# Splitting the activations of a second feed-forward product where they are made, in a hybrid decoder layer on one core

## The chip, the core and the metric

The kernel runs on one core of a Trainium2 chip. The metric is the device time of one execution in microseconds (us). Before the change it is 1844.94 us, the median of three runs (1843.99 to 1846.52).

The engines that matter here are TensorE (PE in the profile, with its weight loads PEld), VectorE (DVE), ScalarE (ACT), GpSimd (POOL) and SyncE (SP), which here issues nearly all transfers, in the order of its instructions.

## The reference, cut to what matters

One decoder layer on 1024 tokens of width 1024: two mixers, a merge, and a SwiGLU feed-forward block with 2816 hidden units, in float32. The change touches only the end of the layer:

```python
x = x + SwiGLU(rms_norm(x))      # (silu(h @ w_gate) * (h @ w_up)) @ w_down
return rms_norm(x)
```

Products are computed to nearly float32 accuracy: each float32 operand is split into two parts of 12 bits, `src = hi + lo`, and TensorE computes hi·hi + hi·lo + lo·hi.

## The kernel before, in words

The order of TensorE's instructions is the order of the code. The order on VectorE, ScalarE, GpSimd and SyncE is laid out by a scheduler when the program is built (but for a stretch ahead of the feed-forward block that is written out by hand), from its own estimates of durations; on the chip each engine goes through its list strictly in order, each instruction waiting for its semaphores.

*Splitting.* `split(hi, lo, src)` (L79) is two instructions: ScalarE writes `hi` (L81), then VectorE subtracts, `lo = src - hi` (L82).

*Gate and up.* The loop `for f in range(NF_)` (L1529) makes 22 tiles of 128 hidden units. Each takes seven products of quarters (Strassen and Winograd), in the order 1, 6, 2, 7, 4, 5, 3. A product is 12 matmuls: four pieces, and for each of them three matmuls (L143 to L145), of which the third takes `alo`, the rest of the split operand. `prepare` splits the operand of a product two products ahead; `ahi` and `alo` have three buffers each. VectorE sums the results; the activations of a tile are `act[0]` (L1547) and `act[1]` (L1559), halves of the tokens. Two tiles make a pair. At the end of the even tile GpSimd computes S3 = A11 - A21 (L1567), at the end of the odd one S1, S2 and S4 (L1571 to L1573; S2 reads S3). Then SyncE stores the seven operands of the second product, 1: A11, 2: A12, 3: S4, 4: A22, 5: S1, 6: S2, 7: S3, as float32 to `act_d` in DRAM (L1575).

*The second product.* `down(p)` (L1610) is called for p = 1, 2, 3, 6, 5, 7, and a last part does p = 4; each has 11 pieces `k` of 12 matmuls. For a piece, `a_load` (L1457) brings the activations back (a transfer of 512 KB holds two pieces, three buffers `raw`), and two splits follow: of the activations (`ahi`, `alo`) and of w_down's quarter (`act` buffers). The loads of w_down (`w_load`, L1451) stand in the same queue. The quarters of w_down are also combined: VectorE forms B12 - B11 in place (L1590), GpSimd the other sums (`psub`, L87, and L1595). The results are added to the rows of x by VectorE and GpSimd between the pieces.

Of the kernel before, what the change touches and what calls it, by code (L numbers as in the profile page):

```python
# [11 lines left out]
F32 = mybir.dt.float32  # L12
# [8 lines left out]
P = 128  # L21
S = 1024
D = 1024
NT = S // P            # token tiles
KD = D // P            # contraction tiles of the model width
H = 4                  # delta-net heads
# [3 lines left out]
SEG0 = 2056            # first column of the sparse-attention part of w_in  # L30
# [3 lines left out]
def tile_hybrid(ctx: ExitStack, tc: tile.TileContext, a: dict, out: bass.AP, dbg=None):  # L34
# [13 lines left out]
    # ------------------------------------------------------------ constants and pools of the whole kernel  # L48
# [18 lines left out]
    # per head a square of 128 x 128, at a pitch by which its blocks of 16 x 16 on the diagonal are evenly spaced  # L67
# [10 lines left out]
    # ------------------------------------------------------------ helpers  # L78
    def split(hi, lo, src):  # L79
        """src = hi + lo, each of 12 bits"""  # L80
        nc.scalar.activation(hi, src, AF.Copy)  # L81
        nc.vector.tensor_tensor(lo, src, hi.bitcast(F32), op=ALU.subtract)  # L82
# [19 lines left out]
    def load_w(parts, cols, spare=False):  # L102
        """parts: (k0, k1, c0, c1, DRAM AP [p1 - p0, k, c], p0, p1) of a piece [128, 8, cols]; its (hi, lo)"""
# [18 lines left out]
    # pieces of weights in the order of their use, each loaded while the one before it is in use  # L122
# [17 lines left out]
    def mmk(ps, a_, b_, first, last):  # L140
        """ps += a^T b of split operands (hi, lo)"""
        (ah, al), (bh, bl) = a_, b_
        nc.tensor.matmul(ps, ah, bh, start=first, stop=False)  # L143
        nc.tensor.matmul(ps, ah, bl, start=False, stop=False)  # L144
        nc.tensor.matmul(ps, al, bh, start=False, stop=last)  # L145
# [10 lines left out]
    def rms_scale(p, src, nfeat, junk):  # L156
        """(mean square + eps)^-0.5 of each row of src [128, n]"""
# [7 lines left out]
    def to_feature_major(ptile, src, dst):  # L165
        """rows of a token tile [128, 1024] into columns; dst(kk) gives (hi, lo) of four feature tiles"""
# [9 lines left out]
    class Model:  # L176
        """rough times of the engines, for the order of TensorE's work"""
# [5 lines left out]
        def run(self, eng, ready, dur):  # L183
            """the end of dur ns of work that can begin at ready; TensorE goes in order, the others where they have time"""
# [16 lines left out]
    def weave(m, streams, filler=None, oldest=False):  # L201
        """emit the streams' steps, of those that can begin first (the one that waits longest, where oldest);
        a stream asks with the time its step is ready"""
# [26 lines left out]
    def steps(m, gen):  # L230
        """a stream of steps that give their (time, time until the next is ready); None: not yet"""
# [12 lines left out]
    # ------------------------------------------------------------ the order of the weights  # L244
# [19 lines left out]
    # ============================================================ phase 1: projections and the delta net  # L264
# [36 lines left out]
    # ---------------- the normed input, and z, beta, alpha: token major  # L301
    with ExitStack() as px:
# [16 lines left out]
        def zproj(s, i, wh, wl):  # L319
# [11 lines left out]
            # twice the silu; the half of it comes with the norm  # L331
# [42 lines left out]
    # ---------------- constants of the delta net  # L374
    upper = gt("upper", [P, P])                       # upper[t, i] = 1 where t <= i
# [7 lines left out]
    # blocks of 16 rows are inverted one by one, then level l joins blocks of b = 2^l rows:  # L383
    # LM[i, l - 4, c] = 1 where i is in an odd block, c in the even one before
    LM = gt("LM", [P, 3, P])
    for l in range(4, 7):
# [4 lines left out]
        # p >= 2 b m + b  # L391
        nc.gpsimd.affine_select(out=v, in_=src, pattern=[[-2 * b, nb], [0, 2 * b]], compare_op=ALU.is_ge,
                                fill=0.0, base=-b, channel_multiplier=1)
        # p < 2 b m + 2 b
        nc.gpsimd.affine_select(out=v, in_=v, pattern=[[2 * b, nb], [0, 2 * b]], compare_op=ALU.is_gt,
                                fill=0.0, base=2 * b, channel_multiplier=-1)
        # c in the even block
# [8 lines left out]
    # ---------------- beta, log decay and its running sum, all tokens at once  # L406
# [13 lines left out]
    # softplus(x) = max(x, 0) + log1p(e), e = exp(-|x|); log1p(e) = 2 artanh(e / (2 + e))  # L420
# [21 lines left out]
    # ---------------- q, k, v of the delta net: feature major, convolution and SiLU (twice its value)  # L442
# [31 lines left out]
    # its columns as rows, to be spread over all partitions  # L474
# [8 lines left out]
    # ---------------- delta net, a chunk of 128 tokens at a time  # L483
# [11 lines left out]
    EV = 1750                        # ns from a step's products to the next step of its chain  # L495

    def prepare_chunks():
        for c in range(NT):
# [4 lines left out]
            # decay: gb[., h, i] = gc_i on every partition  # L503
# [42 lines left out]
            # back to feature major  # L546
# [24 lines left out]
            # A[j, i] = L[i, j] and (q k^T)^T, both with the decay  # L571
# [12 lines left out]
            # the blocks on the diagonal: rows of Y = (I + U)^-1 from the last, U[a, b] the block of A  # L584
# [43 lines left out]
    def scan_chunks():  # L628
        Sst = None
        for c in range(NT):  # L630
# [36 lines left out]
            # gated norm of the heads, transposed  # L667
# [30 lines left out]
    # ---------------- the other projections: sparse attention's token major, merge gates feature major  # L698
# [28 lines left out]
    # ============================================================ phase 2: sparse attention  # L727
    # with the gates and the delta net's branch set in where TensorE would wait
# [6 lines left out]
    KT = [kvt(f"KT{g}", [P, 2, S], F32R) for g in range(2)]      # rows (hi | lo) of the two branches  # L735
    VS = [kvt(f"VS{i}", [P, 2, 2, P], F32R) for i in range(NT)]  # [token, branch, g, halves]
    KCS = kvt("KCS", [P, 2, 64], F32R)                           # rows (hi | lo); [g, block]
# [985 lines left out]
```

## Time and profile before

| | |
|---|---|
| time, median of three runs | 1844.94 us (1843.99 to 1846.52) |
| span of the profiled execution | 1843.4 us |
| TensorE busy | 1731.2 us, 94% |
| VectorE busy | 1201.9 us, 65% |
| ScalarE busy | 786.5 us, 43% |
| GpSimd busy | 794.5 us, 43% |
| mean granted TensorE clock | 0.982 |

The time of the profiled execution is its span, from the first instruction to the last, and a little around it; the timed runs lie 0.6 to 3.1 us above the span. The profile's TensorE line in 40 slices is 9 or more nearly everywhere, so the few slices that are not are where time can be won, and any new wait of TensorE in a slice at 9 is lost time. The second product runs from 1604.41 to 1836.15 us in the trace; what follows are the last sums, the last norm and the stores.

### The profile page before, as it was taken

Reading aid. Unit: us, or ns where it says so; the run is one execution under the profiler, and the core shown is the slowest. Engines: PE = TensorE matmul, PEld = TensorE weight load, DVE = VectorE, ACT = ScalarE, POOL = GpSimd, SP = SyncE. Lnnn points to the kernel's source line nnn. Section 1 sums busy time; section 2 is a strip of 40 time slices with the busy share of each in tenths; the row PEclk is TensorE's granted clock in tenths of the full one; section 3 lists DMA queues with packets and bytes.
Section 4 is the critical chain, followed back from the end, with each engine's and each line's share of the span. In section 5 each row is a group of like instructions: output and inputs, shape, how many; then the busy total and the mean of one; then the engine's idle time right before and its main releaser. Section 6 shows DMA issues by size and latency. Waiting matters only on the chain.

```text
span 1843.4 us, 26137 instructions
## 1 busy us (share of the span) xinstructions
PE 1731.2 (94%) x9252; PEld 1449.0 (79%) x9252; DVE 1201.9 (65%) x2084; ACT 786.5 (43%) x1852; POOL 794.5 (43%) x1118
## 2 busy tenths in 40 slices
PE   7999989999999999999999977799999999989998
PEld 7888888988877777877778756578888888877776
DVE  6566466665443687776734598975555555678985
ACT  5244333433221897877721124433333333334452
POOL 3410243443132875765510564644444343354720
PEclk9999999999999999999999999899999999999999
DMA  6323434443463211011085520033333332662232
GB/s 203 98 92 98 137 115 110 113 124 83 115 189 97 80 47 49 20 44 38 16 262 140 201 84 1 12 115 111 95 103 114 96 111 91 211 240 87 86 136 99
DMA packets 182947, 196.41 MB, mean 107 GB/s; under 512 B 23344, under 2 KB 139296, under 8 KB 182816
## 3 DMA queue, kind: packets, MB, share of 16 engines
q1 hardware_dynamic: 164048, 162.03, 28.7%
q0 software_dynamic: 18560, 32.62, 5.9%
q8 instruction: 73, 1.20, 0.3%
q14 instruction: 58, 0.48, 0.1%
q10 hardware_dynamic: 208, 0.09, 0.0%
HBM read 139.01 MB, written 55.69 MB: 106 GB/s over the span
## 4 chain that ended last, share of the span: by engine, by line
PE 62%; DVE 13%; issue 12%; POOL 6%; ACT 3%; DMA 3%; SPq 0%; POOLq 0%; DVEq 0%; ACTq 0%
PE M L144 13%; PE M L145 12%; PE M L143 12%; PE s L1068 3%; PE ppt L1126 3%; DVE alo L82 2%; PE po L1153 2%; PE po L1154 2%; DVE Ut L592 1%; PE pm L143 1%; PE pm L144 1%; PE pm L145 1%; POOL Ps L1103 1%; PE py L623 1%; DMA E<-gc_d 1%
## 5 line engine op out<-in xcount | busy, mean ns | idle before, releaser
L1073 ACT ACTIVATE Ps<-s,mx 128x384 f32<-128x384 f32 (+3 forms) x192 | 106.1, 561 | 23.5 <-DVE mx L1072 22.4
L81 ACT ACTIVATE ahi<-fraw 128x512 fp32r<-128x512 f32 x88 | 55.7, 633 | 140.5 <-PE M L144 140.5
L82 DVE TENSOR_TENSOR ptl<-ppt,pth 128x512 fp32r<-128x512 f32 (+1 forms) x148 | 99.0, 683 | 25.5 <-ACT pth L81 25.1
L1103 POOL TENSOR_SCALAR Ps<-Ps,cs 128x384 f32<-128x384 f32 (+3 forms) x192 | 108.3, 582 | 13.2 <-ACT pth L81 5.5
L1072 DVE TENSOR_REDUCE mx<-s 128x1 f32<-128x384 f32 (+3 forms) x192 | 95.0, 514 | 19.1 <-PE s L1071 13.5
L1068 PE MATMUL s<-KT,qt 128*128 128x384 f32 (+3 forms) x384 | 99.3, 359 | 3.0 <-DVE ptl L82 1.8
L143 PE MATMUL pn<-whi,h 128*128 128x264 f32 (+1 forms) x320 | 100.4, 314 | 1.1 <-ACT nst L706 1.1
L143 PE MATMUL pm<-h,whi 128*128 128x512 f32 x224 | 97.2, 434 | 0.2 <-ACT thm L719 0.2
L81 ACT ACTIVATE pth<-ppt 128x512 fp32r<-128x512 f32 (+1 forms) x148 | 87.1, 604 | 23.8 <-PE ppt L1126 21.6
L144 PE MATMUL pn<-wlo,h 128*128 128x264 f32 (+1 forms) x320 | 90.9, 284 | 0.0
L145 PE MATMUL pn<-whi,h 128*128 128x264 f32 (+1 forms) x320 | 90.9, 284 | 0.0
L144 PE MATMUL M<-act,ahi 128*128 128x512 f32 x194 | 78.7, 406 | 12.8 <-DVE act L82 12.8
L145 PE MATMUL pm<-h,wlo 128*128 128x512 f32 x224 | 89.7, 400 | 0.0
L144 PE MATMUL pm<-h,whi 128*128 128x512 f32 x224 | 89.2, 398 | 0.0
L82 DVE TENSOR_TENSOR alo<-fraw,ahi 128x512 fp32r<-128x512 f32 x88 | 73.6, 836 | 22.9 <-ACT ahi L81 22.9
L82 DVE TENSOR_TENSOR wlo<-wraw,whi 128x1024 fp32r<-128x1024 f32 (+1 forms) x50 | 61.1, 1232 | 41.9 <-ACT whi L81 40.2
L81 ACT ACTIVATE ahi<-fsum 128x512 fp32r<-128x512 f32 x66 | 41.8, 633 | 105.7 <-PE M L144 105.7
L82 DVE TENSOR_TENSOR alo<-ar,ahi 128x512 fp32r<-128x512 f32 x66 | 68.2, 1033 | 26.6 <-ACT ahi L81 26.6
L81 ACT ACTIVATE ahi<-ar 128x512 fp32r<-128x512 f32 x66 | 41.7, 631 | 100.1 <-PE dn L144 50.7
L81 ACT ACTIVATE whi<-wraw 128x1024 fp32r<-128x1024 f32 (+1 forms) x50 | 52.2, 1060 | 70.7 <-PE pm L144 31.1
L1126 PE MATMUL ppt<-ident,Ps 128*128 128x128 f32 x528 | 77.7, 273 | 1.4 <-POOL Ps L1103 1.1
L145 PE MATMUL M<-act,alo 128*128 128x512 f32 x194 | 76.6, 395 | 0.0
(518 smaller groups left out, 5741.2 us busy)
## 6 DMA issues: line engine op xcount, KB each, us to landing
wraw<-in_w_in_dram SPq DMA_DIRECT2D x50, 512.0 KB, 4.2
fraw<-in_w_gate_up_dram SPq DMA_DIRECT2D x44, 512.0 KB, 4.2
ar<-act_d SPq DMA_DIRECT2D x35, 512.0 KB, 3.5
act_d<-asum SPq DMA_DIRECT2D x44, 256.0 KB, 2.4
act_d<-act SPq DMA_DIRECT2D x33, 256.0 KB, 2.0
gt_d<-thm POOLq DMA_DIRECT2D x32, 256.0 KB, 3.0
gg<-gt_d SPq DMA_DIRECT2D x32, 256.0 KB, 2.7
qkv_d<-ac POOLq DMA_DIRECT2D x24, 256.0 KB, 2.3
```

Source lines behind the costliest of these rows:

```text
L81: nc.scalar.activation(hi, src, AF.Copy)
L82: nc.vector.tensor_tensor(lo, src, hi.bitcast(F32), op=ALU.subtract)
L143: nc.tensor.matmul(ps, ah, bh, start=first, stop=False)
L144: nc.tensor.matmul(ps, ah, bl, start=False, stop=False)
L145: nc.tensor.matmul(ps, al, bh, start=False, stop=last)
L1068: nc.tensor.matmul(s, qt[:, h, l, :], KT[g][:, b, j0 * P + c0:j0 * P + c1], start=l == 0, stop=l == 1 and not ext)
L1072: nc.vector.tensor_reduce(mx[:, h, n:n + 1], s, axis=AX.X, op=ALU.max, negate=True)
L1073: nc.scalar.activation(pr, s, AF.Exp, bias=mx[:, h, n:n + 1], accum_out=sums[:, h, n:n + 1])
L1103: nc.gpsimd.tensor_scalar(v, v, cs[:, h, n:n + 1], 1.0, op0=ALU.mult, op1=ALU.mult)
L1126: nc.tensor.transpose(pt[:k, h, :], prs[h][:, jj * P:jj * P + k], ident)
L1153: nc.tensor.matmul(po, v, th_, start=first, stop=False)
L1154: nc.tensor.matmul(po, v, tl_, start=False, stop=fin is not None)
```

## The change

The seven operands are split when they are made. `a_store(p, t)` writes `hi` to a new tile `ahs` (two buffers), `lo` in the place of the float32 operand, and stores both: two transfers of 256 KB for each operand instead of one. Operand 1 is split and stored at the end of the even tile, the other six at the end of the odd tile, in the order 7, 5, 6, 4, 3, 2. In the second product `a_load` brings both halves of one piece in one transfer of 512 KB, and the split of the activations is gone; w_down's halves now use the buffers `ahi` and `alo`. For the last product the halves are loaded straight into the big tiles. `act` has four buffers instead of six. The comments of the file were taken out as well.

```diff
-    act_d = {p: [dtile(f"act_d{p}_{k}", [P, 2, 512]) for k in range(0, NK, 2)] for p in range(1, 8)}
+    act_d = {p: [dtile(f"act_d{p}_{k}", [P, 2, 512]) for k in range(NK)] for p in range(1, 8)}
...
     def a_load(p, k):
-        if (p, k // 2) not in ars:
-            m = min(2, NK - k)
-            t = fw.tile([P, KD, P], F32, tag="raw", name="ar", bufs=3).rearrange("p (m k) t -> p m (k t)", m=2)
-            nc.sync.dma_start(t[:, :m, :], act_d[p][k // 2][:, :m, :])
-            ars[p, k // 2] = t
+        if (p, k) not in ars:
+            t = fw.tile([P, KD, P], F32R, tag="raw", name="ar", bufs=3).rearrange("p (l k) t -> p l (k t)", l=2)
+            nc.sync.dma_start(t.bitcast(F32), act_d[p][k])
+            ars[p, k] = t
+        return ars[p, k][:, 0, :], ars[p, k][:, 1, :]
...
-        act = [fp.tile([P, 512], F32, tag="act", name=f"act{n}", bufs=6) for n in range(2)]
+        act = [fp.tile([P, 512], F32, tag="act", name=f"act{n}", bufs=4) for n in range(2)]
...
             a_load(1, 0)
+            a_load(1, 1)
...
+        def a_store(p, t):
+            hi = fp.tile([P, 512], F32R, tag="ahs", name="ahs", bufs=2)
+            split(hi, t.bitcast(F32R), t)
+            for l, v in enumerate((hi.bitcast(F32), t)):
+                nc.sync.dma_start(act_d[p][f // 2][:, l, :], v)
...
             nc.gpsimd.tensor_tensor(S3, A11, A21, op=ALU.subtract)
+            a_store(1, A11)
             continue
...
-        for p, t in ((1, A11), (2, A12), (3, S4), (4, A22), (5, S1), (6, S2), (7, S3)):
-            nc.sync.dma_start(act_d[p][f // 4][:, f // 2 % 2, :], t)
+        for p, t in ((7, S3), (5, S1), (6, S2), (4, A22), (3, S4), (2, A12)):
+            a_store(p, t)
...
-            bt_ = (fw, "sum") if (p, k) == (1, 0) else (fp, "act")
-            ah, al, bh, bl = flat(fw, "ahi"), flat(fw, "alo"), *(flat(*bt_) for _ in range(2))
-            split(ah, al, a_side(p, k))
+            bh, bl = flat(fw, "ahi"), flat(fw, "alo")
             split(bh, bl, b_side(p, k))
+            ah, al = a_load(p, k)
...
-        split(ah, al, a_side(4, k))
+        for l, v in enumerate((ah, al)):
+            nc.sync.dma_start(v.bitcast(F32), act_d[4][k][:, l, :])
         split(bh, bl, b_side(4, k))
```

The order of TensorE's instructions stays. Three places where the lists of the other engines change:

VectorE, behind the second activation of an odd tile (`act1`), before the change: each split rest `alo` stands alone between two sums (L1542 and on).

```order
L1559 TENSOR_TENSOR act1_13502<-c1_13499 128x512
L82 TENSOR_TENSOR alo_13681<-fraw_13497,ahi_13680 128x512
L1542 TENSOR_TENSOR c1_13658<-M_13684,c2_13659 128x512
L82 TENSOR_TENSOR alo_13699<-fraw_13497,ahi_13698 128x512
L1543 TENSOR_TENSOR c2_13659<-M_13702,c2_13659 128x512
```

The same place with the change; `asum_13584` is S3 (operand 7), `asum_13737` S1 (operand 5), `asum_13738` S2 (operand 6).

```order
L1561 TENSOR_TENSOR act1_13598<-c1_13595 128x512
L82 TENSOR_TENSOR asum_13584<-asum_13584,ahs_13743 128x512
L82 TENSOR_TENSOR asum_13737<-asum_13737,ahs_13748 128x512
L82 TENSOR_TENSOR alo_13800<-fraw_13593,ahi_13799 128x512
L82 TENSOR_TENSOR asum_13738<-asum_13738,ahs_13753 128x512
L1543 TENSOR_TENSOR c1_13777<-M_13803,c2_13778 128x512
L82 TENSOR_TENSOR alo_13818<-fraw_13593,ahi_13817 128x512
L82 TENSOR_TENSOR act1_13598<-act1_13598,ahs_13758 128x512
L1544 TENSOR_TENSOR c2_13778<-M_13821,c2_13778 128x512
```

The rest for the next tile's product 7 (`alo_13800`) stands behind two of the new subtractions, the one for product 4 (`alo_13818`) behind three.

SyncE's queue at the passage from the last pair of tiles to the second product, before the change; `ar` are the loads of activations, of two pieces each.

```order
L1461 DMA ar_16196<-act_d1_4_12426 128x1024
L1575 DMA act_d4_10_12447<-act1_15954 128x512
L1575 DMA act_d5_10_12453<-asum_16086 128x512
L1575 DMA act_d3_10_12441<-asum_16088 128x512
L1575 DMA act_d6_10_12459<-asum_16087 128x512
L1461 DMA ar_16238<-act_d1_6_12427 128x1024
```

The same with the change, where a load holds one piece; the loads of pieces 0, 1 and 2 stand further ahead.

```order
L1571 DMA act_d7_10_12500<-asum_16264 128x512
L1571 DMA act_d5_10_12478<-ahs_16419 128x512
L1571 DMA act_d5_10_12478<-asum_16408 128x512
L1571 DMA act_d6_10_12489<-ahs_16424 128x512
L1571 DMA act_d6_10_12489<-asum_16409 128x512
L1571 DMA act_d4_10_12467<-ahs_16429 128x512
L1571 DMA act_d4_10_12467<-act1_16274 128x512
L1571 DMA act_d3_10_12456<-ahs_16434 128x512
L1571 DMA act_d3_10_12456<-asum_16410 128x512
L1571 DMA act_d2_10_12445<-ahs_16439 128x512
L1571 DMA act_d2_10_12445<-act0_16273 128x512
L1461 DMA ar_16507<-act_d1_3_12427 128x1024
```

The load of piece 3 stands behind all eleven remaining stores of the last pair; before, the loads of pieces 0 to 5 stood ahead of the last four stores.

VectorE in product 2 of the second product, with the change; `alo` are now the rests of w_down's quarter, the line L1600 is B12 - B11 in place.

```order
L82 TENSOR_TENSOR alo_16702<-B6h_16451,ahi_16701 128x512
L82 TENSOR_TENSOR alo_16720<-B6h_16451,ahi_16719 128x512
L1600 TENSOR_TENSOR B11l_16369<-B5h_16949,B11l_16369 128x512 x4
L82 TENSOR_TENSOR alo_16740<-B6l_16521,ahi_16739 128x512
L82 TENSOR_TENSOR alo_16758<-B6l_16521,ahi_16757 128x512
L1600 TENSOR_TENSOR B21h_16371<-B5l_17023,B21h_16371 128x512 x3
L82 TENSOR_TENSOR alo_16776<-B6l_16521,ahi_16775 128x512
```

Four of the sums stand together between the rests of pieces 3 and 4, and three between those of pieces 5 and 6; before, two and three of them stood between two pieces there, with two rests for each piece.

## Rows read from the trace of the kernel before

**Rows 1.** Windows: a stretch of gate and up, then products 1, 2, 3, 6, 5, 7

```profile
core 0: us, PE busy (x) PEld busy (x) DVE busy (x) ACT busy (x) POOL busy (x), PEclk, DMA share, GB/s
1440.00:1480.00 40.00, 40.00 (x179) 33.11 (x178) 23.33 (x34) 13.00 (x21) 18.29 (x14) 1.00 0.32 101
1604.41:1634.69 30.28, 30.28 (x133) 24.62 (x132) 18.99 (x27) 15.22 (x27) 6.54 (x5) 1.00 0.92 331
1634.69:1678.23 43.54, 35.60 (x133) 27.20 (x132) 43.54 (x34) 13.19 (x24) 37.08 (x23) 0.88 0.31 107
1678.23:1710.75 32.52, 30.51 (x133) 24.62 (x132) 22.26 (x31) 15.07 (x31) 9.92 (x7) 1.00 0.29 91
1710.75:1743.17 32.42, 31.09 (x133) 24.46 (x132) 31.09 (x27) 12.70 (x23) 23.93 (x15) 1.00 0.27 90
1743.17:1776.15 32.98, 31.46 (x134) 24.39 (x132) 27.77 (x27) 12.83 (x23) 18.85 (x12) 1.00 0.27 88
1776.15:1806.07 29.92, 29.92 (x134) 24.78 (x132) 28.89 (x51) 22.46 (x45) 2.99 (x4) 1.00 0.56 193
```

**Rows 2.** Waits of PE from 1590 us on: us in total, times, longest

```profile
PE M L144 <- DVE act L82: 12.8, 14, 4.0
```

**Rows 3.** Timeline in product 2: start us, us, engine, line, out<-in [idle before <-releaser]

```profile
1646.01 1.71 POOL L1595 TENSOR_TENSOR B6h<-B6h,B11h 128x512 f32<-128x512 f32 x1
...
1646.52 1.75 DVE L82 TENSOR_TENSOR alo<-ar,ahi 128x512 fp32r<-128x512 f32 x1
...
1648.19 1.75 DVE L82 TENSOR_TENSOR act<-B6l,act 128x512 fp32r<-128x512 f32 x1
...
1649.99 0.80 PE L144 MATMUL M<-act,ahi 128*128 128x512 f32 x1 [4.03 <-DVE act L82]
...
1651.01 0.63 PE L143 MATMUL M<-act,ahi 128*128 128x512 f32 x1
```

**Rows 4.** The page's groups: the split of the activations in the second product

```profile
L82 DVE TENSOR_TENSOR alo<-ar,ahi 128x512 fp32r<-128x512 f32 x66 | 68.2, 1033 | 26.6 <-ACT ahi L81 26.6
L81 ACT ACTIVATE ahi<-ar 128x512 fp32r<-128x512 f32 x66 | 41.7, 631 | 100.1 <-PE dn L144 50.7
```

**Rows 5.** Timeline at the end of an odd tile, and the next tile's product 7

```profile
1453.68 0.69 DVE L1559 TENSOR_TENSOR act<-c 128x512 f32<-128x512 f32 x1
1454.45 1.29 POOL L1571 TENSOR_TENSOR asum<-act,act 128x512 f32<-128x512 f32 x1 [7.59 <-DVE act L1559]
...
1455.50 0.79 DVE L82 TENSOR_TENSOR alo<-fraw,ahi 128x512 fp32r<-128x512 f32 x1 [1.13 <-ACT ahi L81]
1455.70 1.74 POOL L1572 TENSOR_TENSOR asum<-act,asum 128x512 f32<-128x512 f32 x1
1457.52 1.29 POOL L1573 TENSOR_TENSOR asum<-act,asum 128x512 f32<-128x512 f32 x1
...
1458.77 1.74 POOL L1416 TENSOR_TENSOR fsum<-fraw 128x512 f32<-128x512 f32 x1
...
1460.71 0.39 PE L145 MATMUL M<-B7h,alo 128*128 128x512 f32 x1
```

**Rows 6.** Timeline at the start of the second product

```profile
1606.01 0.69 DVE L1559 TENSOR_TENSOR act<-c 128x512 f32<-128x512 f32 x1
1606.61 0.69 DVE L82 TENSOR_TENSOR act<-B11h,act 128x512 fp32r<-128x512 f32 x1
...
1606.78 1.67 POOL L1571 TENSOR_TENSOR asum<-act,act 128x512 f32<-128x512 f32 x1 [17.75 <-DVE act L1559]
...
1608.48 1.77 DVE L82 TENSOR_TENSOR act<-B11h,act 128x512 fp32r<-128x512 f32 x1 [1.18 <-POOL asum L1571]
```

**Rows 7.** The page's DMA issues: count, KB each, us from issue to landing

```profile
ar<-act_d SPq DMA_DIRECT2D x35, 512.0 KB, 3.5
act_d<-asum SPq DMA_DIRECT2D x44, 256.0 KB, 2.4
act_d<-act SPq DMA_DIRECT2D x33, 256.0 KB, 2.0
```

More of the change, by code (lines that the diff above doesn't have):

```diff
@@ L1448, in flat @@
     def flat(p, tag, dtype=F32R):
-        return p.tile([P, 4, P], dtype, tag=tag, name=tag, bufs={"act": 6, "asum": 4}.get(tag, 3)).rearrange("p k t -> p (k t)")
+        return p.tile([P, 4, P], dtype, tag=tag, name=tag, bufs={"asum": 4}.get(tag, 3)).rearrange("p k t -> p (k t)")
     def w_load(n, j):
@@ L1598, in b_side @@
         return {1: q11, 2: q21, 3: q22, 5: q11, 7: q22, 4: q21}[p]
-    def a_side(p, k):
-        if k % 2 == 0:
-            a_load(p, k)
-        return ars[p, k // 2][:, k % 2, :]
     def banks_of(p):
```

## The prediction, as it was made before the change was timed

> **What bounds the kernel now.** I read the windows first, by product. In gate and up TensorE is busy for 40.00 of 40.00 us at clock 1.00, while VectorE has 23.33 us of work and ScalarE 13.00 [rows 1]. So nothing can be won there, and a wait put there is lost in full. In the second product, product 7 shows the pace without waits: 132 matmuls in 29.92 us, 0.2267 us each, 2.72 us for a piece of twelve. Against 29.92, product 1 loses 0.36 us, product 2 13.62, product 3 2.60, product 6 2.50 and product 5 3.06, in all 22.1 us. That is all that the change can win. Product 2's loss has two halves: 43.54 - 35.60 = 7.94 us in which TensorE waits, and 35.60 - 29.92 = 5.68 us of matmuls at the lower clock (mean 0.88).
>
> The waits view says for whom: 14 waits, 12.8 us, for VectorE's rest of w_down's half [rows 2]. In product 2 VectorE is busy for all 43.54 us, GpSimd for 37.08. The timeline shows why 0.69 us instructions fill it: there each takes 1.75 us, 1.67 apart, as do GpSimd's beside them [rows 3]. Alone VectorE's follow each other in 0.60 us (1606.01, 1606.61) and GpSimd's in 1.25 (1454.45, 1455.70) [rows 5, 6]. So subtractions of two tiles in SBUF and GpSimd's instructions exclude each other and take turns, about 0.60 and 1.08 us each. Sums that read PSUM aren't held up. A piece then needs two rests, 3.34 us where GpSimd is busy, against TensorE's 2.72.
>
> **What goes.** 77 splits of activations: 66 in products 1 to 7, 68.2 us on VectorE at a mean of 1033 ns, 41.7 us on ScalarE [rows 4], and 11 in the last product, which loses nothing now. One rest for a piece remains: 1.67 us at worst, under 2.72.
>
> Products 6 and 5: 5.56 us lost now. I take 1.0 left, for the loads into the last product's tiles, which SyncE holds until GpSimd has read the old contents (bounds 0 and 3). Gain 4.6.
>
> Products 2 and 3: 16.2 us lost now. Here VectorE also does eleven subtractions B12 - B11, so three a piece become two: 22 x 1.67 = 36.7 us where GpSimd keeps up, and product 2 takes 29.92. In the new order four and then three of them stand together between rests. Four with the rest behind them are 5 x 1.67 = 8.4 us; the three buffers cover two pieces, 5.4 us; so TensorE waits some 3 us there, near 2 at the three, near 1 at the results of product 1, and pays the lower clock behind the first. I take 8 us left, gain 8.2 (bounds: nothing left; two thirds of 16.2, 10.8, left).
>
> Product 1's 0.36 goes as well: its rests were the cause.
>
> **What comes: the load of piece 3.** A buffer now holds one piece, so three pieces are ahead at the start, and piece 3's load is queued on SyncE behind the last pair's stores. These wait for a chain. `act1` ends at 1606.70 [rows 6]. GpSimd then takes S1 and S2, to about 1609.3 (2 x 1.25). VectorE does the rest of operand 7 to 1610.0, S4 takes its turn, the rest of operand 5 ends near 1611.8 (1.08 + 0.60). The half of operand 5 is stored behind operand 7's rest, at 1610.4. Only two `ahs` buffers exist: operand 4's half waits for that store, 2.2 us (between 2.0 and 2.4 [rows 7]), and for the rest of 5: 1612.6, and 0.63 on ScalarE [rows 4]. Its store goes at 1613.4, behind three others; operand 2's half waits for it, 1615.6 to 1616.3; its rest ends at 1617.0, and its store and then piece 3's load are issued by 1617.4. A load takes 3.5 us [rows 7]: 1620.9. TensorE wants piece 3 at 1604.41 + 3 x 2.72 = 1612.57, so it waits 8.4 us, once. Nothing covers this: TensorE's next instructions are this piece's. Behind it come matmuls at the lower clock; where the longest wait was 4.03 us they last 0.63 us each instead of 0.39 [rows 3, 5]. Product 2 pays 5.68 us on 7.94 of waits, the longest being half of these, so I take 2.4 for one wait. Together 10.8 us; bounds 6 (the chain two us shorter, full clock) and 15 (each transfer 1 us longer, 1.5 us more of low clock).
>
> The Trainium skill (DMA: Bandwidth & Descriptors, Anatomy of one DMA) puts a GpSimd-issued transfer at 2.0 us plus its bytes over 436 GB/s, which is an estimate of 2.6 us for 256 KB and 3.2 for 512. By that two stores and the load take 8.4 instead of 7.9 us, and this term is 0.5 more; the measured 2.4 and 3.5 of this trace, issued by SyncE, are used.
>
> **What comes: seven splits for each pair of tiles in gate and up.** ScalarE: 7 x 0.63 us in 38 us, within its idle time. VectorE: 7 x 0.60 alone. The averages hide it, the place does not. Now the rest for product 7 of the next tile is taken at 1455.50, 5 us early; its third matmul wants it at 1460.71 [rows 5]. In the new order two subtractions stand ahead of it, and the first, operand 7's in place, must wait for S2, which reads S3. S2 then starts at 1455.70 with nothing beside it and ends at 1456.99. VectorE's instruction starts 0.03 us behind a GpSimd instruction it waits for (1608.45, 1608.48 [rows 6]), GpSimd's own dependent one 0.08 (1457.44, 1457.52 [rows 5]). So VectorE goes first: 1457.0 to 1457.6; S4 to 1458.7; operand 5's rest to 1459.3; the next tile's sum of L1416 to 1460.4; product 7's rest to about 1461.0. With a weight load, the matmul goes near 1461.3 instead of 1460.71: 0.6 us late. Product 4's rest stands behind three subtractions and a sum, near 1463.9, and adds 0.15. Product 5's and 3's fit. 0.75 us for a pair, ten pairs, 7.5 us; bounds 0 and 35 (below). Even tiles have one subtraction, 0.6 us, and several us of room: nothing.
>
> The Trainium skill (SBUF — State Buffer, SBUF: two separate sides) says that of a VectorE instruction with two SBUF inputs and a GpSimd one, whichever starts first has the shared ports for its whole length. Rows 3 and 5 agree in the lengths (1.75, 0.79 and 1.74 us); by the rule the 0.05 us would decide as above. No run here shows that tie yet.
>
> Transfers: 77 more stores of 256 KB and twice the loads. A load is issued when the piece three ahead is done, 5.4 us early, and takes 3.5. In product 1 the queue moved 331 GB/s already, but there the starvation leaves time. Cost 0, up to 6 below.
>
> Sum: 7.5 + 10.8 - 8.2 - 4.6 - 0.4 = +5.1 us. On the profiled span of 1843.4 that is 1848.5; the timed median is 1.5 above the span, so 1850.
>
> **Rivals.**
> *Cover in gate and up, and in product 2.* If VectorE and GpSimd don't collide as worked out (the sum of L1416 is late by its load, rests come in time) the ten pairs cost 0, product 2 keeps 4 us instead of 8, and the starvation costs 9. For it: 16 us of VectorE and 22 of GpSimd are idle in 40 [rows 1]. Against: the collision sits in a stretch where GpSimd runs five in a row. 9.0 - 12.2 - 4.6 - 0.4 = -8.2: 1837, faster.
> *GpSimd wins the tie.* S4 first puts both rests ahead one turn later; product 7's rest ends at 1462.5, the matmul waits 2.05 us, and some six matmuls 0.2 us longer each follow at the lower clock: 3.3 us a pair, 33 in all: 1844.9 + 5.1 + 25 = 1875. For it: 0.05 us is little. It decides from the point where S4 starts before operand 7's rest.
> *The loads fall behind.* With w_down's loads between them the activations' loads land in 6 instead of 3.5 us, 0.6 late for some ten pieces: +6, 1856. For it: 331 GB/s in product 1. Against: 91 to 107 from product 2 on, where the need is 512 KB in 2.72 us, 193 GB/s.
>
> **Chances.** Forecast 0.52, cover 0.22, tie 0.14, loads 0.12. The forecast's own range is 1842 to 1858, of which slower by over 0.2% (3.7 us, about what a measurement can tell from no change) is 0.32, within 0.17, faster 0.03. Cover adds 0.20 to faster and 0.02 to within; the other two, 0.26, are slower. So faster 0.23, same 0.19, slower 0.58. The range runs from within the cover case to short of the tie's whole price: 1836 to 1868.
>
> **What would show it.** The new profile should have one wait of TensorE of some 8 us in product 1, ended by the load of piece 3 (3 to 11 would still be this step); windows over gate and up at 39 rather than 40 of 40 us busy, with waits of L145 for VectorE's rests of product 7 in every second tile; product 2 at 36 to 40 us instead of 43.5; products 6 and 5 near 30. Wrong I would be if gate and up stays full, or if piece 3's load is issued before 1612, or if product 2 loses as much as before with half of the rests gone.

## The result, and the profile after

The changed kernel takes 1859.47 us (median of four runs, 1855.99 to 1861.09), the kernel before beside it 1845.73. The ratio is 1.0071, with a 95% interval from 1.0057 to 1.0084: slower by 13.7 us, where 5.1 were forecast. A second measurement, below, gives 1.0060 (1.0045 to 1.0075), 10.5 us. The direction is the forecast's; the size is two to nearly three times its, and 1859.47 lies above the forecast's own range (1842 to 1858), though inside the wider one that allows for the rivals. By the stages below, three of the four terms came within 2.5 us of what was worked out, and the gain in products 6 and 5 did not come.

The windows of the changed kernel answer to [rows 1]; the columns are the same. First a stretch of gate and up, then products 1, 2, 3, 6, 5 and 7.

```profile
1455.00:1495.00 40.00, 39.69 (x175) 32.30 (x174) 30.83 (x42) 16.20 (x28) 18.00 (x13) 1.00 0.44 145
1615.63:1658.81 43.18, 32.64 (x134) 26.19 (x132) 17.22 (x22) 12.04 (x20) 8.73 (x6) 0.88 0.91 328
1658.81:1694.35 35.54, 31.31 (x134) 24.46 (x132) 29.56 (x25) 7.54 (x13) 32.98 (x22) 1.00 0.62 206
1694.35:1724.27 29.92, 29.92 (x134) 24.77 (x132) 13.06 (x17) 9.30 (x19) 9.70 (x8) 1.00 0.55 180
1724.27:1757.81 33.54, 30.91 (x134) 24.44 (x132) 13.11 (x18) 6.95 (x11) 19.23 (x15) 1.00 0.77 268
1757.81:1788.74 30.93, 30.46 (x134) 24.47 (x132) 12.85 (x17) 7.70 (x14) 17.27 (x12) 1.00 0.83 280
1788.74:1819.86 31.12, 30.53 (x133) 24.69 (x133) 23.81 (x42) 14.23 (x28) 2.52 (x4) 1.00 0.72 226
```

Gate and up is no longer full (39.69 of 40). The 13.6 us of product 2 have become 5.6, the 2.6 of product 3 nothing. Product 1 has taken their place: 43.18 us instead of 30.28, with the clock at 0.88. Products 6, 5 and 7 lose 3.62, 1.01 and 1.20 against 29.92, 5.8 together, as much as before (5.6).

The waits of TensorE from 1200 us on (us in total, times, longest) answer to [rows 2]. VectorE's rest of w_down was behind 12.8 us there; now activations on their way are behind 14.5.

```profile
PE M L143 <- DMA ar<-act_d: 14.5, 9, 9.6
PE M L145 <- DVE alo L82: 3.2, 10, 0.3
PE M L144 <- DVE alo L82: 3.1, 2, 1.7
```

The end of an odd tile in the timeline, where [rows 5] stood (start, us):

```profile
1461.70 0.69 DVE L1561 TENSOR_TENSOR act<-c 128x512 f32<-128x512 f32 x1
1462.47 1.29 POOL L1581 TENSOR_TENSOR asum<-act,act 128x512 f32<-128x512 f32 x1 [7.36 <-DVE act L1561]
1463.72 1.29 POOL L1582 TENSOR_TENSOR asum<-act,asum 128x512 f32<-128x512 f32 x1
...
1465.04 2.40 DVE L82 TENSOR_TENSOR asum<-asum,ahs 128x512 fp32r<-128x512 f32 x2 [2.65 <-DMA fraw<-in_w_gate_up_dram]
1465.09 1.81 POOL L1583 TENSOR_TENSOR asum<-act,asum 128x512 f32<-128x512 f32 x1
...
1466.85 1.74 POOL L1416 TENSOR_TENSOR fsum<-fraw 128x512 f32<-128x512 f32 x1
1467.36 1.78 DVE L82 TENSOR_TENSOR alo<-fraw,ahi 128x512 fp32r<-128x512 f32 x1
...
1469.19 0.50 PE L145 MATMUL M<-B7h,alo 128*128 128x512 f32 x1 [0.31 <-DVE alo L82]
```

This is the sequence of the prediction: S2, the rests of operands 7 and 5 (one row of two instructions), S4 between them, then the rest for product 7, which ends at 1469.14. TensorE's matmul before it began at 1468.49, so this one begins 0.70 instead of 0.23 us later, and the one behind it another 0.11 late: 0.58 us, and 0.14 more at product 4, which is most of the 0.80 us by which a pair is now longer (38.88 instead of 38.08). The release named beside 1465.04 is the last event in time; the wait was for S2, which ended at 1465.01.

SyncE's queue at the start of the second product, and the matmul that waits:

```profile
1607.50 2.63 SPq L1455 DMA_DIRECT2D B21l<-in_w_down_dram  x1
1621.29 0.34 SPq L1571 DMA_DIRECT2D act_d<-asum  x1
...
1628.54 0.32 SPq L1571 DMA_DIRECT2D act_d<-act  x1
1628.96 1.58 SPq L1461 DMA_DIRECT2D ar<-act_d  x3
1630.61 0.42 SPq L1455 DMA_DIRECT2D B7h<-in_w_down_dram  x1
...
1633.57 0.77 PE L143 MATMUL M<-ahi,ar 128*128 128x512 f32 x1 [9.62 <-DMA ar<-act_d]
```

Behind w_down's load the queue issues nothing from 1610.1 to 1621.3, while the first of the last pair's stores waits for operand 7's rest; the eleven stores are issued from 1621.3 to 1628.5, and the load of piece 3 behind the last of them.

### The profile page after: what moved, and what is told of

It reads as the page before. It is cut to its first block, busy times and chain, and to the rows that moved or that the text cites. A ratio compares the mean times of both kernels' runs of the same rounds, so it can differ in the third digit from the quotient of the medians.

```text
span 1857.0 us, 26467 instructions
## 1 busy us (share of the span) xinstructions
PE 1737.6 (94%) x9252; PEld 1450.9 (78%) x9252; DVE 1206.3 (65%) x2084; ACT 786.6 (42%) x1852; POOL 796.6 (43%) x1118
## 4 chain that ended last, share of the span: by engine, by line
PE 61%; DVE 15%; issue 9%; POOL 5%; DMA 5%; ACT 3%; SPq 0%; DVEq 0%; POOLq 0%; ACTq 0%
PE M L145 10%; PE M L143 10%; PE M L144 10%; DVE alo L82 3%; PE s L1068 3%; PE ppt L1126 3%; PE pq L144 2%; PE pq L143 2%; PE pq L145 2%; PE po L1153 2%; PE po L1154 1%; DMA fraw<-in_w_gate_up_dram 1%; PE pm L143 1%; DMA ar<-act_d 1%; PE pm L144 1%
## 5 line engine op out<-in xcount | busy, mean ns | idle before, releaser
L1103 POOL TENSOR_SCALAR Ps<-Ps,cs 128x384 f32<-128x384 f32 (+3 forms) x192 | 108.6, 587 | 13.8 <-ACT pth L81 5.5
L143 PE MATMUL M<-ahi,ar 128*128 128x512 f32 x198 | 79.2, 400 | 15.4 <-DMA ar<-act_d 14.5
L82 DVE TENSOR_TENSOR alo<-fraw,ahi 128x512 fp32r<-128x512 f32 x88 | 83.8, 952 | 0.4 <-ACT ahi L81 0.4
L144 PE MATMUL M<-alo,ar 128*128 128x512 f32 x198 | 78.1, 394 | 3.1 <-DVE alo L82 3.1
L145 PE MATMUL M<-ahi,ar 128*128 128x512 f32 x198 | 77.9, 393 | 0.0
L144 PE MATMUL pq<-h,whi 128*128 128x512 f32 x192 | 75.6, 394 | 0.0
L143 PE MATMUL pq<-h,whi 128*128 128x512 f32 x192 | 75.5, 393 | 0.0
```

The source lines that it names most:

```text
L1103: nc.gpsimd.tensor_scalar(v, v, cs[:, h, n:n + 1], 1.0, op0=ALU.mult, op1=ALU.mult)
```

## Experiments

All work on the changed kernel. For each I read when product 1 starts after the first result of gate and up (VectorE's `act[0]` of the first tile), and what each product takes more than 29.92 us. All figures are in us, from the timelines of the profiled runs, one profile for each row; the ratio is that of the timed runs:

| kernel | gate and up to product 1 | product 1 loses | 2 and 3 | 6, 5 and 7 | ratio to before |
|---|---|---|---|---|---|
| before | 395.7 | 0.4 | 16.2 | 5.6 | 1 |
| changed | 403.8 | 13.3 | 5.6 | 5.8 | 1.0071 |
| changed, second time | 403.6 | 13.3 | 5.5 | 9.0 | 1.0060 |
| last pair's stores later | 403.6 | 3.0 | 11.8 | 7.7 | 1.0027 |
| other pairs' stores later | 403.6 | 13.8 | 6.5 | 5.8 | 1.0056 |
| both | 403.6 | 2.5 | 10.5 | 5.7 | 1.0024 |
| last loads later | 403.6 | 13.3 | 5.6 | 5.1 | 1.0043 |
| gate and up in written order | 402.7 | 15.1 | 9.2 | 8.1 | 1.0083 |
| second product in written order | 403.7 | 6.9 | 0.1 | 2.7 | 0.9981 |
| both orders | 401.4 | 7.4 | 0.1 | 1.8 | 0.9968 |
| both, transfers spread | 395.7 | 7.4 | 2.0 | 0.6 | 0.9925 |
| gate and up from the third tile | 395.7 | 14.5 | 8.8 | 6.3 | 1.0054 |
| both, transfers even | 395.7 | 0.9 | 1.5 | 3.2 | 0.9912 |

By the rows of the first profile, unrounded, the change costs 8.05 + 24.71 - 22.14 = 10.6 us; by those of the second 7.87 + 27.84 - 22.14 = 13.6. The two medians gave 13.7 and 10.5. So the cost is known to some 3 us: the first profile carries 3.2 us from ahead of gate and up, the second 0.9 from there and 3.2 more in product 6. A gain of a few us between two medians is therefore checked against the stages below.

### The changed kernel once more

No edit.

> The changed kernel once more, unaltered, for a second profile: ahead of gate and up its first profile was 3.2 us behind the kernel before, in code that the change doesn't touch. My theory (this differs from run to run): another offset, within 4 us of zero to either side, while gate and up to product 1 takes 403.8 us and the second product 234 us again, within 1 us each. Rival (the changed program is slower ahead of gate and up, for instance by its place in memory): 2.5 to 4 us behind again.

Measured: 1856.81 us, 1.0060 (1.0045 to 1.0075). The first result of gate and up came at 1209.60 us, 0.9 behind the 1208.70 of before; in the first profile it was 1211.87. In the ten profiles of changed kernels in which all engines go through the same instructions in the same order up to there, as in the kernel before, it lies between 0.9 us ahead and 3.2 behind. So that offset is the run's, not the change's. Gate and up repeats within 0.2 us. The second product doesn't repeat within 1 us, as I had written: it took 237.4 instead of 234.3 us, and the difference is product 6 (36.79 instead of 33.54).

### The last pair's stores inside product 1

```
-        for p, t in ((7, S3), (5, S1), (6, S2), (4, A22), (3, S4), (2, A12)):
-            a_store(p, t)
+        late += [partial(a_store, p, t) for p, t in ...]      # other pairs: at once
 def down(p, load=None):
+            if p == 1 and k >= 3:      # behind piece k
+                for g in late[:1]:
+                    g()
+                del late[:1]
```

> The last pair's six splits and twelve stores are issued inside product 1, one operand behind each piece from the fourth on, so that the load of piece 3 stands ahead of all but one of them on SyncE's queue. My theory (the load is late because it is queued behind the stores): it is issued near 1619 instead of 1629 us on the changed kernel's clock, TensorE's wait of 9.6 us and the low clock behind it go, product 1 takes 30 to 31.5 us instead of 43.2, and the time falls by 11 to 13 us, from 1859.5 to about 1847. Rival (w_down's loads ahead of it, or the transfer itself, hold it): a wait of 5 us or more stays in product 1, time above 1853.

Measured: 1851.6 us, 1.0027 (1.0013 to 1.0041). The wait of 9.6 us is gone and product 1 takes 32.91 us: the queue's order was its cause. (30 to 31.5 were expected; short waits for activations are left.) But of the 10.3 us that product 1 gave back, 8.1 were lost again behind it, 6.2 of them in products 2 and 3. The median fell by 7.9 us; by the profiles' stages the gain is 2.2, and 3.8 us lie ahead of gate and up, where nothing was altered. Product 3 in a window, then the queue, VectorE and TensorE up to there:

```profile
1678.41:1716.23 37.82, 32.44 (x133) 25.84 (x133) 23.86 (x23) 9.29 (x19) 22.08 (x15) 0.95 0.45 143
```

```profile
1637.10 6.85 SPq L1461 DMA_DIRECT2D ar<-act_d  x3
1644.00 0.43 SPq L1455 DMA_DIRECT2D B7l<-in_w_down_dram  x1
...
1674.62 6.86 DVE L1602 TENSOR_TENSOR B11l<-B5h,B11l 128x512 f32<-128x512 f32 x4
...
1686.10 5.16 DVE L1602 TENSOR_TENSOR B21h<-B5l,B21h 128x512 f32<-128x512 f32 x3
...
1692.98 0.67 PE L144 MATMUL M<-alo,ar 128*128 128x512 f32 x1 [2.73 <-DVE alo L82]
```

While TensorE waited 9.6 us, w_down's loads had run ahead: `B7l` was issued at 1631, 15.5 us after product 1's start. Now they stand behind loads that wait for their buffers, and `B7l` comes 32.4 us after it. B12 - B11 for the last seven pieces then falls into product 3, in rows of four and three at 1.7 us each beside GpSimd, and TensorE waits for the rests behind them.

### The other pairs' stores inside the next tile

```
         def prod(n):
-            return early.get((f, n)) or product(...)
+            bank = early.get((f, n)) or product(...)
+            if f % 2 == 0 and n != 1:
+                for s in late[:1]:
+                    s()
+                del late[:1]
+            return bank
```

> The stores and splits of every pair of tiles but the last are issued inside the next tile, one behind each of its products from the second on, so that only one subtraction instead of two stands ahead of the split for product 7 on VectorE. My theory (the order at the odd tile's end makes the stall): the wait of 0.32 us at product 7's third matmul goes, a pair takes 38.08 us again instead of 38.89, ten pairs give 8 us, 1859.5 becomes about 1851.5; product 1 keeps its wait of 9.6. Rival (seven more splits for a pair cost as such, wherever they stand, because VectorE and GpSimd take turns): pairs of 38.6 us or more, 1857 or above.

Measured: 1857.33 us, 1.0056 (1.0043 to 1.0069). A pair still takes 38.87 us. Yet the place of the stall has moved:

```profile
1463.96 0.69 DVE L82 TENSOR_TENSOR asum<-asum,ahs 128x512 fp32r<-128x512 f32 x1 [2.65 <-POOL asum L1588]
1464.01 1.80 POOL L1589 TENSOR_TENSOR asum<-act,asum 128x512 f32<-128x512 f32 x1
1464.58 1.79 DVE L82 TENSOR_TENSOR alo<-fraw,ahi 128x512 fp32r<-128x512 f32 x1
...
1466.29 3.48 DVE L82 TENSOR_TENSOR asum<-asum,ahs 128x512 fp32r<-128x512 f32 x2
...
1470.29 0.68 DVE L82 TENSOR_TENSOR alo<-fraw,ahi 128x512 fp32r<-128x512 f32 x1
...
1471.02 0.50 PE L145 MATMUL M<-B4h,alo 128*128 128x512 f32 x1 [0.49 <-DVE alo L82]
```

The rest for product 7 now comes second, in time. The scheduler put the rests of operands 5 and 6 right behind it, two turns with GpSimd, and now product 4's rest is late: its matmul begins 0.88 instead of 0.23 us behind the one before it, 0.65 us late, where product 7's had been 0.47 late. So the number didn't tell my theory from its rival. Only a kernel with none of these subtractions in that room could.

### Both deferrals

The two edits above together.

> Both deferrals together. If the two losses are independent the gains add: 12 + 8 = 20 us, 1839.5, which is 6 us faster than before the change. Rival (the time given back is lost elsewhere: product 2 starts earlier and its w_down quarter or the activations' loads come later against it): 1843 to 1847, with product 2 or 3 above 36 us.

Measured: 1850.51 us, 1.0024 (1.0014 to 1.0035). The rival's case, and more: gate and up still takes 403.6 us, and 10.5 us are lost in products 2 and 3, of which 8.3 in product 3. The time lies above both cases.

### The last product's loads later

```
+    sp = ctx.enter_context(tc.manual_schedule(engines={mybir.EngineType.SP}))
     for t, y in down(6):
...
+            if p == 7:                 # in down, behind piece k
+                last_load(0, k)        # half of operand 4
+                if k >= 4:
+                    last_load(1, k - 4)   # its rest
```

> Only the order on SyncE's queue in products 6, 5 and 7 is changed: it issues in written order, and the 22 loads into the last product's tiles are written inside product 7 instead of being taken up from product 6 on. My theory (SyncE holds the activations' loads while it waits for GpSimd to finish with B5h): the waits of 1.9, 0.4, 0.3 and 0.25 us for activations in products 6, 5 and 7 go, the three lose about 1 us (the 0.7 us wait for ScalarE's half stays) instead of 5.8, time falls by 4.5 us to 1855. Rival (the transfers themselves fall behind, 512 KB for each piece): the waits stay or move into product 7, where more now stands on the queue, time 1858 to 1862.

Measured: 1854.39 us, 1.0043 (1.0031 to 1.0055). First what SyncE's queue waits for in the changed kernel from 1700 us on, then products 6, 5 and 7 of this one.

```profile
SPq L1684 <- POOL B4h L88: 5.1, 1, 5.1
SPq L1684 <- POOL B7l L88: 5.0, 1, 5.0
SPq L1684 <- POOL B7h L88: 3.8, 1, 3.8
```

```profile
1720.68:1750.60 29.92, 29.92 (x133) 24.77 (x132) 14.52 (x18) 6.96 (x11) 20.12 (x15) 1.00 0.60 195
1750.60:1780.52 29.92, 29.92 (x133) 24.77 (x132) 13.30 (x17) 7.49 (x12) 17.30 (x12) 1.00 0.61 200
1780.52:1815.58 35.06, 31.06 (x134) 24.46 (x132) 24.02 (x43) 14.29 (x30) 2.52 (x4) 1.00 0.98 356
```

Products 6 and 5 now lose nothing (the 0.7 us for ScalarE went as well), so the last product's loads, or SyncE's order around them, were the cause of their 4.6 us. And these 22 loads beside the pieces and results fill the transfers of product 7 (share 0.98), which loses 5.1 instead of 1.2: by the stages 0.7 us are won, and that the median lies where my theory put it is luck. The edit takes the holds and the bytes out of products 6 and 5 together, so it doesn't tell which of the two was the cause there. The trace of the changed kernel does for the longest wait of product 6:

```profile
1730.90 0.32 SPq L1461 DMA_DIRECT2D ar<-act_d  x1
1736.34 0.32 SPq L1684 DMA_DIRECT2D B5h<-act_d  x1
1736.75 0.38 SPq L1461 DMA_DIRECT2D ar<-act_d  x1
...
1740.94 0.47 PE L143 MATMUL M<-ahi,ar 128*128 128x512 f32 x1 [1.92 <-DMA ar<-act_d]
```

Loads of activations are issued 2.72 us apart when nothing holds them. This one came 5.85 us behind the last, after the hold of 5.0 us, and so was 3.1 late. The hold of 3.8 us ends 1.1 us ahead of product 6, the one of 5.1 us within it, and behind that TensorE lost only some 0.1 us. The shorter waits of products 5 and 7, 0.1 to 0.4 us, follow no hold of this length: their loads were on the way for 5.4 us or more.

### Gate and up in written order

```
+    dve = tc.manual_schedule(engines={mybir.EngineType.DVE})
+    dve.__enter__()
...
+            if n in ((4, 5, 3), (6, 2, 7, 4))[f % 2] and late:
+                late.pop(0)()          # one store, behind product n
```

> Only gate and up: VectorE issues in written order there, and of a pair's seven splits one stands behind each of the products 4, 5, 3 of the next even tile and 6, 2, 7, 4 of the odd one, so that none comes between the odd tile's end and the next tile's split for product 4. The deferral by one tile that was tried before left a pair at 38.88 us: the wait had only moved from product 7 (0.47 us late) to product 4 (0.65 late). My theory (three subtractions of the stores, taking turns with GpSimd's S4 and the first two sums of the next tile, are more than the room there): with none of them in that room the pairs take 38.08 us, gate and up give 8 us back, the time is about 1851.5, 0.3% above the kernel before. Rival (seven splits cost 0.8 us a pair wherever they stand): pairs of 38.6 us or more, 1857 or above.

Measured: 1861.16 us, 1.0083 (1.0056 to 1.0109), slower than expected. The pairs do take 38.08 us. But a wait of 3.5 us came in the second tile, where the written order has VectorE finish a sum and a product before a rest that TensorE needs (with the slower matmuls behind it and a shorter wait it takes 7.0 us of the 8), and the last pair's stores fell otherwise: the second product lost 32 us instead of 25.

```profile
PE M L145 <- DVE alo L82: 3.5, 1, 3.5
```

The same with the written order from the third tile on:

> The changed kernel with gate and up alone in the new order, from the third tile on; the first two tiles and the second product stand as the scheduler puts them. My theory (the 0.8 us a pair come from the stores' three subtractions in the room before product 4): pairs of 38.08 us, no wait of 3.5 us at the start, and from the first result of gate and up to product 1 some 396 us as before the change instead of 403.8. Rival (another wait of the written order takes the gain, as the stall at its start did when it began with the first tile): 400 us or more.

Measured: 1855.68 us, 1.0054 (1.0032 to 1.0076). From the first result to product 1 it takes 395.71 us, the same as the kernel before to the hundredth, with all seven splits and stores still there. This settles it: the 8 us were the order of VectorE's list, not the work.

```profile
1455.00:1495.00 40.00, 40.00 (x178) 33.14 (x177) 30.55 (x41) 16.98 (x30) 19.09 (x13) 1.00 0.44 145
```

The second product lost 29.5 us here, and so the gain of 8 shows only in part.

### The second product in written order

```
+        if p == 1:                     # behind piece k
+            if k in (0, 2, 4): w_load(21, k // 2)
+            if k in (6, 8, 10): w_load(22, (k - 6) // 2)
...
+        if p in (2, 3) and n % 2 == 0: # n counts the pieces of both
+            w_one(n // 2)              # 256 KB of the fourth quarter
+            if n: t1(n // 2 - 1)       # B12 - B11 of one piece
```

> Only the second product: SyncE's queue is in written order; the last pair's stores stand in product 1 behind piece 3; w_down's quarters for products 2 and 3 are loaded inside product 1, the fourth quarter in eleven loads of 256 KB, one for two pieces of products 2 and 3, with B12 - B11 of that piece behind it; the last product's loads stand one by one in products 5 and 7, and the stores of results one or two pieces later. My theory (all losses left in the second product come from one queue that holds loads behind other instructions' waits, and from subtractions that then stand in clumps): products 1 to 7 lose at most 8 us together instead of 24.7, time about 1842, below the kernel before. Rival (the transfers themselves are too slow, since each piece now takes 512 KB beside w_down): waits for activations stay in products 1 to 3 and the loss is 14 us or more, 1849 or above.

Measured: 1840.87 us, 0.9981 (0.9972 to 0.9991). Products 2, 3, 6 and 5 lose 0.13 us together: with B12 - B11 one at a time, VectorE keeps up with GpSimd beside it. The 9.6 us that are left, where 8 at most were expected, are in products 1 and 7, at 350 and 318 GB/s.

### Both orders

> Both orders, of gate and up and of the second product, in one kernel. If each does what is expected of it and they add: 1859.5 - 8 - 17 = 1834.5, some 11 us or 0.6% faster than the kernel before. Rival (what gate and up gives back is lost in product 1, which then starts nearer to its loads): 1842 or above.

Measured: 1838.54 us, 0.9968 (0.9954 to 0.9981), between the two cases. Product 1 in windows:

```profile
1607.88:1645.21 37.33, 32.79 (x134) 25.44 (x132) 15.55 (x22) 12.74 (x21) 6.92 (x5) 0.95 1.03 394
```

VectorE, ScalarE and GpSimd are idle for more than half of it; the 16 transfer engines are full (share 1.03).

### Transfers spread, then even

> As the kernel with both orders, but VectorE's written order begins with the third tile (its stall of 3.5 us was in the second), and the transfers that stood together in product 1 (DMA share 1.03, 394 GB/s there) and in product 7 (0.90, 324 GB/s) are spread: two of the last pair's six stores in each of products 1, 2 and 3, w_down's second quarter for product 3 from product 1's end on, the last product's loads one for a piece from product 6 to 7; GpSimd's differences for product 5 stand in product 3 and those for product 7 in product 6. My theory (what is left in products 1 and 7 is transfers queued together, 7.4 and 1.7 us): product 1 loses 2 us or less, product 7 under 1, gate and up's first tiles 4 us less: 1838.5 - 10 = 1828.5. Rival (512 KB a piece is what SyncE's queue can't deliver in 2.72 us, wherever the rest stands): product 1 keeps 5 us or more and the others begin to wait, 1834 or above.

Measured: 1832.94 us, 0.9925 (0.9911 to 0.9940). Gate and up and product 7 as expected; product 1 was missed, with 7.4 us lost at a mean of only 296 GB/s, and products 2 and 3 lost 1.0 each, as the rival says. In product 1 3.1 us were one wait, for a piece's load that stood behind 1 MB of w_down (`B7h`) and two stores: issued at 1628.09, it was there 8.7 us later.

```profile
1624.86 0.43 SPq L1457 DMA_DIRECT2D B7h<-in_w_down_dram  x1
...
1625.93 0.47 SPq L1586 DMA_DIRECT2D act_d<-asum  x1
1628.09 3.04 SPq L1467 DMA_DIRECT2D ar<-act_d  x2
...
1636.78 0.76 PE L143 MATMUL M<-ahi,ar 128*128 128x512 f32 x1 [3.14 <-DMA ar<-act_d]
```

The mean hid a queue again. So the last edit takes these apart:

```
-            if k in (0, 3, 6): w_load(21, k // 3)
-            if k == 9: w_load(22, 0)
+            w_one(k, 21)               # 256 KB behind each piece of product 1
+        if p == 2: w_one(k, 22)        # and of product 2
```

> As the kernel with the transfers spread, where product 1 still lost 7.4 us (a wait of 3.1 behind 1 MB of w_down, and of 0.6 and 0.3), but w_down's quarters for products 2 and 3 are loaded in pieces of 256 KB, one for each piece of product 1 and of product 2, and the last pair's six stores are further apart (products 1, 2, 3 and three in 6). Each piece then has 768 KB in product 1 and about 900 in product 2, 290 and 340 GB/s, where 394 was the most that was moved. My theory (a load of 1 MB ahead of a piece's own load makes that load late): product 1 loses 2 us or less and product 2 no more than 1, 1832.9 - 5 = 1828. Rival (512 KB a piece beside any other stream is too much for the queue): 5 us or more lost in products 1 and 2 together, 1832 or above.

Measured: 1830.30 us, 0.9912 (0.9895 to 0.9928), 16 us faster than the kernel before. Products 1, 2, 6 and 7, and TensorE's waits from 1200 us on:

```profile
1605.72:1636.55 30.83, 30.58 (x134) 24.54 (x133) 13.15 (x18) 10.29 (x17) 4.38 (x4) 1.00 0.90 314
1636.55:1667.64 31.09, 30.48 (x134) 24.62 (x132) 25.23 (x22) 8.18 (x14) 29.09 (x19) 1.00 0.94 324
1697.90:1729.94 32.04, 30.95 (x134) 24.46 (x132) 17.00 (x18) 7.47 (x12) 22.46 (x16) 1.00 0.87 290
1760.30:1790.84 30.54, 30.24 (x134) 24.63 (x132) 23.83 (x43) 14.29 (x30) 2.52 (x4) 1.00 0.80 263
```

```profile
PE M L143 <- DMA ar<-act_d: 2.0, 7, 0.5
PE M L144 <- DVE B6l L82: 1.6, 1, 1.6
```

The wait of 1.6 us lies ahead of the first result of gate and up. Product 1 moves 314 GB/s and loses 0.9 us, where 296 GB/s cost 7.4 when it stood in lumps. Product 2 loses 1.2, a little over the 1 expected, and product 6, to which three stores were moved, 2.1 instead of nothing. The loads' sizes and the stores' places were altered together, so their shares aren't told apart. And no run has the kernel before with these orders: how much of the 16 us is the split's own, and how much the orders would have given without it, is not shown.

## Why the prediction was right, and where it was wrong

*Gate and up: right, 7.5 predicted, 8.05 measured.* Mechanism, place and parts came out: 0.58 us at product 7 (0.6) and 0.14 at product 4 (0.15) for a pair. The tie that I left open went to VectorE, in the row 1463.96 above: it started 0.05 us ahead and took 0.69 us as it does alone, and GpSimd's S4 took 1.80 instead of 1.29. This is the rule of the Trainium skill that the prediction weighed (SBUF — State Buffer, SBUF: two separate sides), and these rows agree with it. The rival in which GpSimd wins the tie, 1875, is out. That the order alone makes the loss is shown by the kernel that gives all of it back with the work unchanged.

*The load of piece 3: right in kind, 10.8 predicted, 13.3 measured in product 1.* It was issued 13.3 us after product 1's start; I had 13.0. TensorE had it 4.6 us later instead of 3.5, with three loads issued in 1.6 us and w_down's behind them (that this is the reason is argued, not shown); the wait is 9.6 instead of 8.4. The matmuls behind it, 0.63 us each for a while at a mean clock of 0.88, and the restarts cost 2.7 (32.64 - 29.92) instead of 2.4, and one more load was 0.9 late. Moving the stores took the wait away. In the working, a store is put at 2.2 us, not at the 2.4 that the paragraph behind it names; with 2.4 for both stores the wait would have come out 0.4 longer.

*Products 2 and 3: better than predicted.* 5.6 of 16.2 us are left, where I had taken 8. All of it is in product 2: 4.2 us of waits (35.54 - 31.31), two for VectorE's rests, 1.5 and 1.7 us long where I had 3, 2 and 1, and three for loads of activations, 1.1 us together, which I had not; and 1.4 us around these five waits, at clock 1.00: I had counted on the lower clock, and it did not fall. (Such restarts are also in the 5.68 us that the prediction calls matmuls at the lower clock.)

*Products 6, 5 and 7: wrong.* The failed step is "I take 1.0 left, for the loads into the last product's tiles", with 0 for the transfers and for product 7. 5.8 us are left, 9.0 in the second profile; products 6 and 5 alone have 4.6, above my bound of 3. The hold on SyncE was the one I named, but its 1.0 was taken, not worked out: it comes three times, for 3.8, 5.0 and 5.1 us, and of the 5.4 us that three buffers cover a transfer of 4.3 takes most. So a load can be held back about 1 us unseen (an estimate from these two); the one above was 3.1 late and cost 1.9. The rest of these products' loss is shorter waits and restarts, most of it for loads on the way (and one of 0.7 us for ScalarE). What the change removed there, VectorE's lateness, was replaced by lateness of the loads: gain 4.6 predicted, -0.3 measured.

*The transfers: a rival that was partly right.* I had set their cost at nothing, and 6 in the rival. I had also read 91 to 107 GB/s behind product 1, where [rows 1] has 88 to 107 and 193 in product 7. Beside piece 3's wait the changed kernel has eight for activations, 4.9 us together (14.5 - 9.6), near the rival's ten of 0.6; of these, 1.9 are the hold's, and a load took 4.3 us, not 6. Product 7's 1.2 us are of this kind. In the kernels without the other losses the transfers bind product 1 at 0.94 to 1.03 of all transfer engines' time. Twice the bytes for each piece was a cost covered by waits elsewhere; as these went, it came up.

Sum: 8.05 + 12.9 - 10.6 + 0.3 = +10.6, against +5.1, by the first profile. Of the difference, 4.9 are products 6, 5 and 7, 2.5 product 1, 0.6 gate and up, and -2.4 products 2 and 3, an error in the other direction that hid part of the first.

## What to carry to other kernels

Work moved out of a starved stage into one where TensorE has no idle time must fit the room at its place, and a mean load of 58% [rows 1] says nothing about that: here the same seven splits cost 8 us in one order and nothing in another. A change that trades arithmetic for loads must be priced on the queue too: list, for each load that a matmul needs, what stands ahead of it and what that waits for, and take from the buffers' lead the transfer's own time, as measured under that load, before calling a hold hidden. And when a wait is removed, look for what ran during it: the weights that were asked for during those 9.6 us were late once it was gone.

## What had not been expected of the hardware

The time ahead of gate and up, with the same instructions in the same order, differed from profile to profile by 4.1 us (the first result of gate and up came at 1207.81 to 1211.87 us). So differences of 0.2% between two profiles say little unless the place is read.

A load of 512 KB landed in a median of 3.5 us before [rows 7] and in 4.3 in the changed kernel, with the same size and queue (the page's DMA issues, last column). It isn't the number of bytes alone: the same 66 loads took 3.5 where the last product's loads were moved into product 7, and 4.7 in the fastest kernel, where TensorE waited 2.0 us for them in all.

```profile
ar<-act_d SPq DMA_DIRECT2D x66, 512.0 KB, 4.3
```

What was issued just ahead of a needed load told more than the mean: a mean of 314 GB/s over product 1 cost 0.9 us with w_down in pieces of 256 KB, and one of 296 cost a wait of 3.1 us with 1 MB in one piece and two stores ahead.
